# Softmax times values on one core: values of four heads in one load, results of two heads in one store, and another order of the queue

## The chip, the cores and the metric

The kernel runs on one core of one Trainium2 chip. The metric is the device time of one execution in microseconds (us); a median of several executions is quoted with the lowest and highest. Every execution quoted here was fast, that is within 1.5% of the fastest of the same kernel. The span in a profile is that of one profiled execution, from its first to its last instruction, and is about 2 us shorter than the device time of the same execution.

## The reference

```python
# scores: [8, 12, 1024, 1024] float32, v: [8, 12, 1024, 64] float32
def reference(scores, v):
    scores_max = np.max(scores, axis=-1, keepdims=True)
    attn = np.exp(scores - scores_max)
    attn = attn / (np.sum(attn, axis=-1, keepdims=True) + 1e-8)
    return np.matmul(attn, v).astype(np.float32)
```

There are 96 heads. Per head 4 MB of scores and 256 KB of values are read and 256 KB of results are written.

## The kernel before

A loop pass takes four heads. For each head one load brings the values (128 partitions x 2 KiB) and one the scores (128 x 32 KiB). ScalarE (ACT) takes the exponential of two rows per partition at a time and writes it as f16. TensorE (PE) transposes these with an identity into PSUM, VectorE (DVE) copies the transposed row out of PSUM (128 x 1024 f16, 0.69 us), and PE multiplies it with the values. These have a column of ones beside them, so the product brings the row sums too. DVE divides by the sums, and one store per head writes the result.

```python
# s_bufs: 4 x [P, R, SK] f32, v_bufs: 4 x [P, C, D] f32, psO_bufs: 4 x [P, G, M] f32 (PSUM)
def finish(u):                       # one row of a head: products, and after each 4 rows the division
    ...
    if g == G - 1:
        ...
        nc.vector.reciprocal(out=recip[:], in_=psO[:, :, D : D + 1])
        nc.vector.tensor_tensor(out=st["out_sb"][:, r - G + 1 : r + 1, :],
                                in0=psO[:, :, 0:D], in1=recip[:].to_broadcast([P, G, D]), op=mult)
    if r == R - 1:
        dma = nc.sync.dma_start(out=one(out_bh, n), in_=st["out_sb"][:])
        ...
        queue(dma)                   # all transfers stand on one queue, in the order of these calls

def load(k, n, parts=(R,), **cond):
    queue(nc.sync.dma_start(out=v_bufs[k][:], in_=one(v_bh, n), **cond))
    ...                              # then the scores of head n, in one piece or several

def heads(n0):
    for k in range(AHEAD):           # AHEAD = 4 heads
        nc.gpsimd.tensor_copy(out=vones_bufs[k][:, :, 0:D], in_=v_bufs[k][:])
        for r in range(R):           # R = 8 rows per partition
            ...                      # exponential, 8 transposes, copy pt <- psT
            if r == R - 1:
                load_next(k, n0)     # k = 0, 1: loads of heads 0, 1 of the next pass
            ...                      # finish() of the row two before
    load_last(n0)                    # loads of heads 2, 3 of the next pass
```

In the last pass but one the last two score loads are cut into pieces of (4, 4) and (2, 2, 2, 2) rows, so that the last exponentials needn't wait for a whole head.

The softmax here doesn't subtract the row's maximum and nothing guards it: scores larger than these inputs give would overflow.

## Time and profile before

| | before |
|---|---|
| time, median of 4 runs | 1068.95 us (1068.76 to 1069.76) |
| span of the profiled run, granted clock | 1066.77 us, 0.845 |
| transfers in a loop pass of four heads | 12 |
| length of a pass in the middle | 43.9 us |
| last packet of scores ended | 1056.87 us |
| from there to the end of the span | 9.90 us |

The lines of the page that carry this stand in the prediction. In the busy shares, an engine near 100% would be the bound. Here only the DMA engines are, so the middle of the program is paid by the packet. The last two rows of the table are about another stretch: after the last packet nothing is transferred but results.

### The profile page before, as it was taken

How to read it: one execution, taken by the hardware profiler on the slowest of the kernel's cores; microseconds unless marked ns; L12 is line 12 of the kernel's file. 1: busy time of each engine (PE TensorE's matmuls, PEld its weight loads, DVE VectorE, ACT ScalarE, POOL GpSimd, SP SyncE). 2: the span in 40 equal slices, each digit the busy share in tenths (PEclk: the TensorE clock that was granted, in tenths of full speed). 3: DMA queues.
4: the chain of work that ended last, by engine and by line, in shares of the span. 5: the costliest groups of instructions: out<-in, count | busy, mean ns of one | idle time of the engine just before them, and what ended most of it. 6: DMA issues, size and time to landing. Idle time of an engine off the chain costs nothing.

```text
span 1066.8 us, 32321 instructions
## 1 busy us (share of the span) xinstructions
PE 762.6 (71%) x12288; PEld 722.4 (68%) x12288; DVE 609.8 (57%) x1157; ACT 736.3 (69%) x432; POOL 59.9 (6%) x102
## 2 busy tenths in 40 slices
PE   3766767677776777668686777767776777767777
PEld 3766766677776767667676767767666677767766
DVE  2655555555564655656565565655555555555556
ACT  4757676676867768577676766677766767667686
POOL 0000000000000000000000000000000000000000
PEclk9888888878888888987888798887898788888889
DMA  9999999999999999999999999999999999999996
GB/s 402 424 425 426 432 431 421 437 434 424 429 430 435 423 440 428 430 429 420 439 430 433 424 432 435 430 423 427 436 433 424 439 422 429 428 439 429 431 423 265
DMA packets 42051, 453.05 MB, mean 425 GB/s; under 512 B 4672, under 2 KB 4672, under 8 KB 29248
## 3 DMA queue, kind: packets, MB, share of 16 engines
q1 hardware_dynamic: 42048, 453.00, 99.8%
q8 instruction: 3, 0.05, 0.0%
HBM read 436.73 MB, written 25.17 MB: 433 GB/s over the span
## 4 chain that ended last, share of the span: by engine, by line
DMA 49%; PE 20%; PEld 9%; ACT 8%; DVE 7%; issue 3%; SPq 3%; DVEq 0%; ACTq 0%
DMA s_nat<-in_scores_dram 49%; PE psT L190 13%; ACT p_nat L182 8%; PE psO L105 7%; PEld L190 6%; DVE pt L196 5%; PEld L105 3%; DVE out_sb L117 2%; SPq L140 1%; SPq L124 1%; SPq L144 1%; DVE recip L116 0%; SPq L166 0%; DVEq L196 0%; ACTq L182 0%
## 5 line engine op out<-in xcount | busy, mean ns | idle before, releaser
L182 ACT ACTIVATE p_nat<-s_nat 128x2048 f16<-128x2048 f32 (+1 forms) x408 | 705.5, 1800 | 253.5 <-DMA s_nat<-in_scores_dram 130.6
L190 PE MATMUL psT<-ident,p_nat 128*128 128x128 f16 x6144 | 583.9, 254 | 257.0 <-ACT p_nat L182 256.1
L196 DVE COPY pt<-psT 128x1024 f16<-128x1024 f16 x768 | 519.2, 690 | 429.2 <-PE L190 138.2
L190 PEld LDWEIGHTS <-p_nat 128*128 128x128 f16 x6144 | 501.3, 154 | 274.9 <-ACT p_nat L182 271.1
L105 PE MATMUL psO<-vones,pt 128*128 128x65 f16 x6144 | 375.8, 205 | 41.8 <-DVE pt L196 37.5
L105 PEld LDWEIGHTS <-pt 128*128 128x128 f16 x6144 | 309.0, 107 | 64.0 <-DVE pt L196 60.3
L175 POOL CAST vones<-v_sb 128x512 f16<-128x512 f32 x96 | 59.2, 617 | 987.7 <-PE L105 443.7
L117 DVE TENSOR_TENSOR out_sb<-psO,recip 128x256 f32<-128x256 f32 x192 | 80.8, 421 | 4.2
L182 ACT ACT_TABLE_LOAD x24 | 30.8, 1283 | 69.6 <-DMA s_nat<-in_scores_dram 64.8
L116 DVE RECIPROCAL recip<-psO 128x4 f32<-128x4 f32 x192 | 33.4, 174 | 18.0 <-PE psO L105 18.0
L57 DVE MEMSET vones<- 128x8 f16 x4 | 0.2, 65 | 0.8 <-PEq L226 0.8
L51 DVE CAST ident<-ident 128x128 f16<-128x128 f32 x1 | 0.2, 228 | 0.3 <-POOL ident masks.py:199 0.3
masks.py:199 POOL TENSOR_SCALAR_AFFINE_SELECT ident<-ident 128x128 f32<-128x128 f32 x1 | 0.3, 293 | 0.1
masks.py:197 POOL MEMSET ident<- 128x128 f32 x1 | 0.2, 204 | 0.3 <-POOLq L226 0.3
L226 POOL MEMSET const-float32-0.0<- 128x1 f32 x1 | 0.1, 98 | 0.2 <-issue 0.2
L226 POOL MEMSET const-bfloat16-1.0<- 128x1 bf16 x1 | 0.1, 101 | 0.0
L226 POOL MEMSET const-uint8-127<- 128x1 uint8 x1 | 0.1, 101 | 0.0
L226 POOL MEMSET const-float32-1.0<- 128x1 f32 x1 | 0.1, 98 | 0.0
## 6 DMA issues: line engine op xcount, KB each, us to landing
s_nat<-in_scores_dram SPq DMA_DIRECT2D x96, 4096.0 KB, 27.1
v_sb<-in_v_dram SPq DMA_DIRECT2D x98, 256.0 KB, 20.6
out_dram<-out_sb SPq DMA_DIRECT2D x96, 256.0 KB, 18.0
s_nat<-in_scores_dram SPq DMA_DIRECT2D x2, 2048.0 KB, 19.9
s_nat<-in_scores_dram SPq DMA_DIRECT2D x4, 1024.0 KB, 18.7
```

What stands on the lines that cost most here:

```text
L51: nc.vector.tensor_copy(out=ident16[:], in_=ident32[:])
L105: nc.tensor.matmul(out=psO[:, g, :], lhsT=pt[:, c * P : (c + 1) * P], rhs=st["vones"][:, c, :], start=(c == 0), stop=(c == C - 1),)
L116: nc.vector.reciprocal(out=recip[:], in_=psO[:, :, D : D + 1])
L117: nc.vector.tensor_tensor(out=st["out_sb"][:, r - G + 1 : r + 1, :], in0=psO[:, :, 0:D], in1=recip[:].to_broadcast([P, G, D]), op=mybir.Al ...
L124: dma = nc.sync.dma_start(out=one(out_bh, n), in_=st["out_sb"][:])
L140: queue(nc.sync.dma_start(out=v_bufs[k][:], in_=one(v_bh, n), **cond))
L144: nc.sync.dma_start(out=s_bufs[k][:, r : r + rows, :], in_=one(sc_bh, n)[:, r : r + rows, :], **cond,)
L175: nc.gpsimd.tensor_copy(out=vones_bufs[k][:, :, 0:D], in_=v_bufs[k][:])
L182: nc.scalar.activation(out=p_nat[:, g : g + rows, :], in_=s_bufs[k][:, r + g : r + g + rows, :], func=EXP,)
L190: nc.tensor.transpose(out=psT[:, c * P : (c + 1) * P], in_=p_row[:, c, :], identity=ident16[:],)
L196: nc.vector.tensor_copy(out=pt[:], in_=psT[:])
L226: nc = _bacc.Bacc("TRN2", target_bir_lowering=False, num_devices=1)
```

## The change

The intent was to spend fewer, larger packets on values and results, and to keep loads from standing behind stores in the queue. Values of four heads come in one load of 128 x 8 KiB, results leave in stores of 128 x 4 KiB for two heads. The queue of a pass is then: scores 0, scores 1, store of heads 0 and 1, scores 2, values, scores 3, store of heads 2 and 3. That is 7 transfers instead of 12.

The larger packets come at a price in layout. A value load now puts each head on 32 partitions, so after one cast on GpSimd (POOL) 16 DVE copies of 32 x 512 spread a pass's values to their places. A result row pair shares a partition, so the identity of the transposes is permuted and each division writes its two halves of partitions separately.

```diff
-    v_bufs = buffers(sb_pool, AHEAD, [P, C, D], FP32, "v_sb")
+    v_sb = sb_pool.tile([P, S, C, D], FP32, name="v_sb")
+    v_half = sb_pool.tile([P, S, C, D], FP16, name="v_half")
...
-    out_bufs = buffers(sb_pool, 4, [P, R, D], FP32, "out_sb")
+    out_bufs = buffers(sb_pool, 2, [P, T, R, D], FP32, "out_sb")
...
-    psO_bufs = buffers(ps_pool, 4, [P, G, M], FP32, "psO")
+    psO_bufs = buffers(ps_pool, 2, [P, R // G, 512], FP32, "psO")
...
+    def normalise(k, st, first, last):
+        psO = st["psO"][:, first:last, 0 : G * M].rearrange("p b (g m) -> p b g m", m=M)
...
+        for t in range(T):
+            part = slice(t * W, (t + 1) * W)
...
+            nc.vector.tensor_tensor(
...
+        if k == AHEAD - 1:
+            if g == G - 1:
+                normalise(k, st, b, b + 1)
+        elif r == R - 1:
+            normalise(k, st, 0, R // G)
+        if r == R - 1 and k == T - 1:
+            store(n0, 0)
...
+    def spread_v(k):
+        for s in range(S):
+            nc.vector.tensor_copy(
+                out=vones_bufs[k][s * Q : (s + 1) * Q, :, 0:D],
+                in_=v_half[k * Q : (k + 1) * Q, s],
+            )
...
-            loads((R,), (R,))
+            load(AHEAD - 2, (n0 + (2 * AHEAD - 2)) % BH)
+            load_v((n0 + 2 * AHEAD) % BH)
+            load(AHEAD - 1, (n0 + (2 * AHEAD - 1)) % BH)
+            store(n0, AHEAD - T)
...
-                loads((4, 4), (2, 2, 2, 2))
+                load(AHEAD - 2, BH - 2, (4, 4))
+                load(AHEAD - 1, BH - 1, (2, 2, 2, 1, 1))
+                store(n0, AHEAD - T)
```

More of the change, by code (lines that the diff above doesn't have):

```diff
@@ L36 @@
     AHEAD = 4
+    Q = P // AHEAD
+    S = P // Q
+    T = 2
     sc_bh = scores.rearrange("b h (p r) j -> (b h) p r j", p=P)
-    v_bh = v.rearrange("b h (p c) d -> (b h) p c d", p=P)
-    out_bh = out.rearrange("b h (p r) d -> (b h) p r d", p=P)
+    v_bh = v.rearrange("b h (i t) d -> (b h i) (t d)", i=Q)
+    W = P // T
+    out_bh = out.rearrange("b h (j x) d -> (b h j) (x d)", j=W)
     const_pool = ctx.enter_context(tc.tile_pool(name="const", bufs=1))
@@ L49 @@
     make_identity(nc, ident32)
-    ident16 = const_pool.tile([P, P], FP16, name="ident16")
-    nc.vector.tensor_copy(out=ident16[:], in_=ident32[:])
+    order16 = const_pool.tile([P, P], FP16, name="order16")
+    nc.vector.tensor_copy(
+        out=order16[:].rearrange("p (t j) -> p t j", t=T),
+        in_=ident32[:].rearrange("p (j t) -> p t j", t=T),
+    )
     vones_bufs = []
     for k in range(AHEAD):
-        vo = const_pool.tile([P, C, M], FP16, name=f"vones{k}")
-        nc.vector.memset(vo[:, :, D : D + 1], 1.0)
+        vo = const_pool.tile([P, C, D + 2], FP16, name=f"vones{k}")
+        nc.vector.memset(vo[:, :, D : D + 2], 1.0)
         vones_bufs.append(vo)
@@ L65 @@
     s_bufs = buffers(sb_pool, AHEAD, [P, R, SK], FP32, "s_nat")
-    v_bufs = buffers(sb_pool, AHEAD, [P, C, D], FP32, "v_sb")
+    v_sb = sb_pool.tile([P, S, C, D], FP32, name="v_sb")
+    v_half = sb_pool.tile([P, S, C, D], FP16, name="v_half")
     p_bufs = buffers(sb_pool, 8, [P, EB, SK], FP16, "p_nat")
     pt_bufs = buffers(sb_pool, 4, [P, SK], FP16, "pt")
-    out_bufs = buffers(sb_pool, 4, [P, R, D], FP32, "out_sb")
-    rc_bufs = buffers(sb_pool, 4, [P, G, 1], FP32, "recip")
+    out_bufs = buffers(sb_pool, 2, [P, T, R, D], FP32, "out_sb")
+    rc_bufs = buffers(sb_pool, 2, [P, R // G, G, 1], FP32, "recip")
     psT_bufs = buffers(ps_pool, 4, [P, SK], FP16, "psT")
-    psO_bufs = buffers(ps_pool, 4, [P, G, M], FP32, "psO")
+    psO_bufs = buffers(ps_pool, 2, [P, R // G, 512], FP32, "psO")
     turn = {}
@@ L95, in one @@
         return bh[bass.ds(n, 1)].rearrange("o p r d -> (o p) r d")
-    def finish(u):
-        n, r, pt, st = u
-        g = r % G
-        if g == 0:
-            st["psO"] = take(psO_bufs)
-        psO = st["psO"]
+    def normalise(k, st, first, last):
+        psO = st["psO"][:, first:last, 0 : G * M].rearrange("p b (g m) -> p b g m", m=M)
+        recip = st["recip"][:, first:last]
+        nc.vector.reciprocal(out=recip, in_=psO[:, :, :, D : D + 1])
+        h = k % T
+        for t in range(T):
+            part = slice(t * W, (t + 1) * W)
+            rows = st["out_sb"][h * W : (h + 1) * W, t, first * G : last * G, :]
+            nc.vector.tensor_tensor(
+                out=rows.rearrange("j (b g) d -> j b g d", g=G),
+                in0=psO[part, :, :, 0:D],
+                in1=recip[part].to_broadcast([W, last - first, G, D]),
+                op=mybir.AluOpType.mult,
+            )
+    def finish(u):
+        n0, k, r, pt, st = u
+        b, g = r // G, r % G
+        if r == 0:
+            st["psO"], st["recip"] = take(psO_bufs), take(rc_bufs)
+            st["out_sb"] = out_bufs[k // T]
         for c in range(C):
             nc.tensor.matmul(
-                out=psO[:, g, :],
+                out=st["psO"][:, b, g * M : (g + 1) * M],
                 lhsT=pt[:, c * P : (c + 1) * P],
-                rhs=st["vones"][:, c, :],
+                rhs=st["vones"][:, c, 0:M],
                 start=(c == 0),
@@ L111, in finish, with store @@
             )
-        if g == G - 1:
-            if r == G - 1:
-                st["out_sb"] = take(out_bufs)
-            recip = take(rc_bufs)
-            nc.vector.reciprocal(out=recip[:], in_=psO[:, :, D : D + 1])
-            nc.vector.tensor_tensor(
-                out=st["out_sb"][:, r - G + 1 : r + 1, :],
-                in0=psO[:, :, 0:D],
-                in1=recip[:].to_broadcast([P, G, D]),
-                op=mybir.AluOpType.mult,
-            )
-        if r == R - 1:
-            dma = nc.sync.dma_start(out=one(out_bh, n), in_=st["out_sb"][:])
-            for other in stores:
-                apart(dma, other)
-                apart(other, dma)
-            apart(dma, dma)
-            stores.append(dma)
-            queue(dma)
+        if k == AHEAD - 1:
[5 more added lines that the diff above has]
+            store(n0, 0)
+    def store(n0, k):
+        rows = out_bh.rearrange("(m x) y -> m x y", x=P)
+        dma = nc.sync.dma_start(
+            out=rows[bass.ds((n0 + k) // T, 1)].rearrange("o x y -> (o x) y"),
+            in_=out_bufs[k // T][:].rearrange("x t r d -> x (t r d)"),
+        )
+        for other in stores:
+            apart(dma, other)
+            apart(other, dma)
+        apart(dma, dma)
+        stores.append(dma)
+        queue(dma)
     stores = []
@@ L139, in load @@
     def load(k, n, parts=(R,), **cond):
-        queue(nc.sync.dma_start(out=v_bufs[k][:], in_=one(v_bh, n), **cond))
         r = 0
@@ L150, in load, with load_v, cast_v @@
             r += rows
+    def load_v(n):
+        rows = v_bh.rearrange("(m x) y -> m x y", x=P)
+        queue(
+            nc.sync.dma_start(
+                out=v_sb[:].rearrange("x s c d -> x (s c d)"),
+                in_=rows[bass.ds(n // AHEAD, 1)].rearrange("o x y -> (o x) y"),
+            )
+        )
+    def cast_v():
+        nc.gpsimd.tensor_copy(out=v_half[:], in_=v_sb[:])
+    def spread_v(k):
+        for s in range(S):
+            nc.vector.tensor_copy(
+                out=vones_bufs[k][s * Q : (s + 1) * Q, :, 0:D],
+                in_=v_half[k * Q : (k + 1) * Q, s],
+            )
     def load_next(k, n0):
@@ L155, in load_next, with last @@
             load(k, (n0 + (AHEAD + k)) % BH, cond=n0 < BH - AHEAD)
-    def load_last(n0):
+    def last(n0):
         before = queued[-1:]
-        def loads(parts2, parts3):
+        with tc.If(n0 < BH - 2 * AHEAD) as cmp:
             queued[:] = before
-            load(AHEAD - 2, (n0 + (2 * AHEAD - 2)) % BH, parts2)
-            load(AHEAD - 1, (n0 + (2 * AHEAD - 1)) % BH, parts3)
-        with tc.If(n0 < BH - 2 * AHEAD) as cmp:
-            loads((R,), (R,))
+            load(AHEAD - 2, (n0 + (2 * AHEAD - 2)) % BH)
+            load_v((n0 + 2 * AHEAD) % BH)
+            load(AHEAD - 1, (n0 + (2 * AHEAD - 1)) % BH)
+            store(n0, AHEAD - T)
         with cmp.Else():
-            with tc.If(n0 < BH - AHEAD):
-                loads((4, 4), (2, 2, 2, 2))
+            with tc.If(n0 < BH - AHEAD) as cmp2:
+                queued[:] = before
+                load(AHEAD - 2, BH - 2, (4, 4))
+                load(AHEAD - 1, BH - 1, (2, 2, 2, 1, 1))
+                store(n0, AHEAD - T)
+            with cmp2.Else():
+                queued[:] = before
+                store(n0, AHEAD - T)
     def heads(n0):
         for k in range(AHEAD):
-            nc.gpsimd.tensor_copy(out=vones_bufs[k][:, :, 0:D], in_=v_bufs[k][:])
+            spread_v(k)
             st = dict(vones=vones_bufs[k])
@@ L182, in heads @@
                         nc.scalar.activation(
-                            out=p_nat[:, g : g + rows, :],
-                            in_=s_bufs[k][:, r + g : r + g + rows, :],
+                            out=p_nat[:, g : g + rows, :].rearrange(
+                                "p r (s v) -> p s r v", s=S
+                            ),
+                            in_=s_bufs[k][:, r + g : r + g + rows, :].rearrange(
+                                "p r (i s c) -> p s (r i) c", s=S, c=C
+                            ),
                             func=EXP,
@@ L192, in heads @@
                         in_=p_row[:, c, :],
-                        identity=ident16[:],
+                        identity=order16[:],
                     )
@@ L198, in heads @@
                     load_next(k, n0)
-                pending.append((n0 + k, r, pt, st))
+                pending.append((n0, k, r, pt, st))
                 if len(pending) > LAG:
@@ L203, in heads @@
             finish(pending.pop(0))
-        load_last(n0)
-    assert BH % AHEAD == 0 and BH >= 2 * AHEAD
+        cast_v()
+        last(n0)
+    assert BH % AHEAD == 0 and BH >= 2 * AHEAD and SK == Q * S * C
+    load_v(0)
     for k in range(AHEAD):
         load(k, k)
+    cast_v()
+    load_v(AHEAD)
     with tc.For_i(0, BH, AHEAD, iteration_sync="reg_based") as n0:
```

## The prediction

> **What bounds the kernel now.** I read the page's busy shares and its DMA lines first, then the busy time by stretch, the trace's packet records (start, duration and size of every DMA packet), the order of issue on the queue, and last the timeline of the final ten microseconds.
>
> ```profile
> PE 762.6 (71%) x12288; PEld 722.4 (68%) x12288; DVE 609.8 (57%) x1157; ACT 736.3 (69%) x432; POOL 59.9 (6%) x102
> ...
> DMA  9999999999999999999999999999999999999996
> ...
> DMA packets 42051, 453.05 MB, mean 425 GB/s; under 512 B 4672, under 2 KB 4672, under 8 KB 29248
> ...
> q1 hardware_dynamic: 42048, 453.00, 99.8%
> ```
>
> No compute engine is above 71%, while the 16 DMA engines are full in 39 of 40 slices. The packet counts tell what travels: 4672 packets of 4 bytes (16 completions for each of 292 transfers), 29248 - 4672 = 24,576 packets of 2 KiB (values and results, one per partition and head), and 12,800 larger ones (scores, nearly all of 32 KiB).
>
> ```profile
> 500.00:544.00 44.00, 32.51 (x516) 30.72 (x515) 25.37 (x48) 30.78 (x19) 2.47 (x4) 0.81 1.01 429
> 544.00:588.00 44.00, 32.57 (x516) 31.00 (x514) 25.56 (x48) 30.77 (x19) 2.47 (x4) 0.81 1.01 430
> 1000.00:1044.00 44.00, 32.04 (x520) 30.45 (x519) 25.69 (x49) 32.61 (x20) 2.47 (x4) 0.84 1.01 430
> 1044.00:1067.00 23.00, 15.18 (x284) 13.84 (x281) 14.47 (x29) 13.10 (x8) 0.62 (x1) 0.94 0.58 239
> ```
>
> In this table of stretches (busy time of PE, its weight loads, DVE, ACT, POOL, then granted clock, DMA share, GB/s) one loop pass of four heads takes 44 us. The DMA share is 1.01 and the rate 429 to 430 GB/s in each pass; both fall only in the last 23 us. Adding up the packet records gives the same: no idle engine time between 50 and 1050 us, some 7 us per engine in all, nearly all of it after the last score load. So the long middle can shrink only if fewer nanoseconds of packets are put on the engines; a wait taken from a compute engine there is worth nothing.
>
> The order of issue on the queue shows what the change wants to mend:
>
> ```profile
> 1013.30 0.34 SPq L140 DMA_DIRECT2D v_sb<-in_v_dram  x1
> 1014.15 0.33 SPq L144 DMA_DIRECT2D s_nat<-in_scores_dram  x1
> 1014.75 10.07 SPq L124 DMA_DIRECT2D out_dram<-out_sb  x3
> 1025.56 0.35 SPq L140 DMA_DIRECT2D v_sb<-in_v_dram  x1
> ```
>
> Three stores are issued one after the other, over 10 us in which no load is issued. Yet the engines don't run dry, as the shares show: score loads of about 9.7 us each (8 packets of 1.21 us on each engine) still stand in front.
>
> The end hangs on the last landing, which the last two one-row exponentials await:
>
> ```profile
> 1057.39 2.01 ACT L182 ACTIVATE p_nat<-s_nat 128x1024 f16<-128x1024 f32 x2 [0.63 <-PE L105]
> ...
> 1060.96 0.43 PE L105 MATMUL psO<-vones,pt 128*128 128x65 f16 x8 [0.28 <-DVE pt L196]
> 1061.65 0.18 DVE L116 RECIPROCAL recip<-psO 128x4 f32<-128x4 f32 x1 [0.75 <-PE psO L105]
> 1061.87 0.42 DVE L117 TENSOR_TENSOR out_sb<-psO,recip 128x256 f32<-128x256 f32 x1
> ```
>
> The name PE in the first line is the last releaser that the profile saw; the last 8 KiB packet ended at 1056.87, half a microsecond before, so I read it as that DMA's completion. From 1057.4 to the end (1066.8) are 9.4 us: two exponentials, transposes, copy, products, normalising, one store.
>
> **What the Trainium skill says.** "DMA: Bandwidth & Descriptors", section Where 436 GB/s comes from, puts the ceiling of the 16 engines at 435 GB/s. The trace agrees: the packet durations grow by (1213 - 84) ns over (32768 - 2048) bytes, which is 27.2 bytes per ns an engine, 435 GB/s for 16. The same page, section Why small descriptors are slow (HBM only), tells of a fixed overhead of about 3 cycles a packet. The trace agrees in kind: 2 KiB packets follow each other at 80 ns (84 recorded, some 4 overlapped), where 2048 bytes at 27.2 take 75.3; so 4.7 ns a packet, whatever its size (32 KiB at 1209 to 1210 ns fits too). "ScalarE: Activation LUTs", section What ACT_TABLE_LOAD costs, gives an activation one element a cycle plus a constant, 186 + 0.833 x 2048 = 1892 ns; the trace has 1901 ns. "VectorE: DVE Perf Modes", section What auto-detection actually checks, says that a 16-bit one-source copy within SBUF takes the fastest mode; no copy of that kind is in this trace, so the price of the new value copies is an estimate from it.
>
> **The change part by part.**
>
> *Values.* 96 loads of 128 x 2 KiB become 24 of 128 x 8 KiB: 12,288 packets become 3072. Per engine 576 fewer packets x 4.7 ns = 2.7 us. The bytes stay.
>
> *Results.* 96 stores of 128 x 2 KiB become 48 of 128 x 4 KiB. The last 4 heads' stores are issued after the last load in both kernels, so up to the last landing 92 x 128 packets become 46 x 128: 5888 / 16 = 368 fewer per engine x 4.7 = 1.7 us.
>
> *Completions.* 72 + 46 = 118 transfers fewer before the last landing, one score piece more: 117 x 5.5 ns (the spacing of the 4-byte packets) = 0.6 us.
>
> So the last landing should come 5.0 us sooner. As a check, one pass of the loop on one engine: before 32 x 1209.5 + 64 x 80 + 12 x 5.5 = 43.89 us, 430 GB/s, as measured; after 38.70 + 8 x 305.9 ns + 16 x 155.3 ns + 7 x 5.5 ns = 43.67 us, or 432 GB/s, 0.22 us a pass.
>
> *Order of the queue.* Score loads of heads 2 and 3 no longer wait behind the stores. That gives the queue more lead, but there was no idle DMA time for it to take away: 0 us.
>
> *Compute.* POOL casts once per pass instead of four times, the same elements: nothing. DVE gains 16 copies of 32 x 512 f16 per pass. The page's fastest mode gives 512 / 4 / 0.96 = 133 ns, with start some 0.2 us (estimate): 384 x 0.2 = 77 us. In the compiled order all 16 stand at the top of the pass, about 3 us before the first copy out of PSUM. The multiply is split over two halves of the partitions: the measured 421 ns for 256 elements is 267 at one element a cycle plus 154, so 512 elements should take 0.69 us. 144 x 0.69 + 96 x 0.42 = 140 us instead of 81; reciprocals fall from 33 to about 21. DVE goes from 610 to about 610 + 77 + 59 - 12 = 734 us, 69%: still below the DMA, and the 3 us at the top fit in the 11 us or so per pass in which PE idles. ACT reads in runs of 8 elements in another order, with as many elements: 1.9 us as before.
>
> *Tail.* The last score piece is one row instead of two, so one exponential (1.0 us) moves before the last landing. The last head's half is normalised by two multiplies instead of one: +0.4 us. The last store carries two heads: 8 packets of 155 ns on each engine instead of 80: +0.6 us. Sum 0.0: 9.4 us stay.
>
> Sum: 1068.9 - 5.0 + 0.0 = **1063.9 us**, 0.5% faster.
>
> **The rivals.** *Stores next to loads cost more than their packets,* so that keeping them apart gains more. Against it: the 2 KiB packets, loads and stores alike, take 84 ns with hardly an exception; records over the usual duration add up to only 1.5 us per engine, all in the first 65 us. If even that vanished, the time would be 1061 to 1062. *DVE becomes the bound or delays PE,* because the copies run in a slower mode and stand at the top. In the slowest (0.7 us each) they would take 11 us per pass, DVE would be near 85 to 90%, and score buffers would come free late; four score buffers with 27 us from issue to landing absorb some of it. It would make 1070 to 1090; I give it little. *ACT's reordered reading is slower.* With 33 us in 44 it can bear some 30% before it binds; no page or row of this trace speaks for a penalty. At double duration the time would be over 1400. *The tail differs:* some engines finish their last 8 KiB packet almost 2 us after others, which could move the end either way by about 1.5 us.
>
> **Range and chances.** The DMA saving is arithmetic on measured packets (4.5 to 6 us); the early stalls and the unequal engines give about 2 us either way, the tail about 1. So 1060.5 to 1067.0. Faster by 2% would mean 1047.5: the bytes alone at 435 GB/s take 1041, and start and tail add over 10, so almost no chance, 1%. Slower by 2% needs a compute rival: 2%.
>
> **What would show it.** Right: DMA share about 1.01 and 432 GB/s in a middle pass, about 22,000 data packets instead of 37,376, no idle DMA in the middle, a DVE share near 69%, value copies near 0.2 us. Wrong: a DMA share under 0.99 in a middle pass (a compute engine or the queue starves it), 4 KiB packets that take clearly over 159 ns or 8 KiB over 309, exponentials over 1.95 us, or a stretch from last landing to end that isn't near 9.4 us.

## The result

| | before | after | predicted |
|---|---|---|---|
| median | 1068.95 us (4 runs) | 1069.66 us (4 runs, 1069.47 to 1070.16) | 1063.9 (1060.5 to 1067.0) |
| pass in the middle | 43.9 us | 43.67 us | 43.67 us |
| last score packet ended | 1056.87 us | 1050.62 us | 5.0 us sooner |
| from there to the end | 9.90 us | 17.39 us | 9.4 us, unchanged |

The last two score pieces of the changed kernel have one row each and travel in packets of 4 KiB; its last 8 KiB packet ended at 1048.13 (the expectation of e1, with "some 8 us sooner", rests on that one). The prediction's 9.4 us start half a microsecond after the last packet, with the exponentials.

The ratio after to before is 1.0006, with a 95% interval of 0.9989 to 1.0023: the same time. Ratios here are the mean time of one kernel's fast runs over that of the other's of the same rounds, so they are not quite the ratio of the medians quoted. "Same" had a chance of 0.97, so the class came true; the time lies 5.8 us above the predicted one and outside the range.

The first view is the page of the changed kernel: its busy shares, the row of DMA busy tenths, and the packets.

```profile
PE 745.1 (70%) x12288; PEld 706.6 (66%) x12288; DVE 775.8 (73%) x1517; ACT 736.0 (69%) x432; POOL 48.1 (5%) x31
...
DMA  9999999999999999999999999999999999999994
...
DMA packets 24916, 453.06 MB, mean 424 GB/s; under 512 B 2768, under 2 KB 2768, under 8 KB 9168
...
q1 hardware_dynamic: 24912, 453.00, 98.8%
```

The change did what it meant to do to the transfers: 22,144 packets with data (24,912 - 2768) instead of 37,376, and the DMA engines are still full in 39 of 40 slices. DVE rose from 57% to 73%.

The next view is busy time by stretch (PE, weight loads, DVE, ACT, POOL, granted clock, DMA share, GB/s), for two passes in the middle of the changed kernel.

```profile
484.00:528.00 44.00, 31.43 (x512) 29.93 (x512) 32.37 (x64) 30.66 (x18) 1.90 (x1) 0.81 1.00 430
528.00:572.00 44.00, 30.78 (x512) 28.97 (x512) 32.61 (x64) 30.67 (x18) 1.90 (x1) 0.84 1.00 430
```

The DMA engines stay the bound there: a share of 1.00, as before. The packet records show no idle time in the middle, 4 KiB packets of 159 ns and 8 KiB packets of 309 ns. The middle was predicted right. What changed in a pass is DVE: 32.4 us of busy time instead of 25.4.

The queue's timeline of the changed kernel shows the new order in one pass.

```profile
961.82 0.34 SPq L175 DMA_DIRECT2D s_nat<-in_scores_dram  x1
962.51 0.33 SPq L187 DMA_DIRECT2D v_sb<-in_v_dram  x1
973.51 0.33 SPq L175 DMA_DIRECT2D s_nat<-in_scores_dram  x1
980.01 0.36 SPq L153 DMA_DIRECT2D out_dram<-out_sb  x1
989.16 5.18 SPq L175 DMA_DIRECT2D s_nat<-in_scores_dram  x2
```

In the place where the kernel before issued three stores in a row, one store now lies between the scores of head 3 (973.51) and the next pass's scores (989.16).

So the loss is at the end. A pass begins with a table load on ACT, once the pass's first scores have landed. In ACT's timeline this is the last one of the kernel before:

```profile
1023.54 1.28 ACT L182 ACT_TABLE_LOAD   x1 [2.77 <-DMA s_nat<-in_scores_dram]
```

and this the last one of the changed kernel, with most of what ACT does afterwards:

```profile
1020.51 1.28 ACT L240 ACT_TABLE_LOAD   x1 [3.45 <-DMA s_nat<-in_scores_dram]
...
1030.19 22.19 ACT L240 ACTIVATE p_nat<-s_nat 128x2048 f16<-128x2048 f32 x13 [1.07 <-DMA s_nat<-in_scores_dram]
```

The last pass starts 3.03 us sooner. Then 13 exponentials run for 22.19 us with at most 0.1 us between them. The last landing, for which the kernel before waited, is no longer in the chain: the last exponential ends at 1052.38, and DVE copies that row out of PSUM only from 1060.22, 7.8 us later. In the kernel before these are 1059.39 and 1060.21.

What is in the chain is DVE. In the kernel before, its first copy of the last pass was:

```profile
1027.89 0.69 DVE L196 COPY pt<-psT 128x1024 f16<-128x1024 f16 x1 [3.43 <-PE L190]
```

In the changed kernel (DVE's timeline, with one line of PE's between) the last pass starts and ends so:

```profile
1024.77 5.04 DVE L199 COPY vones<-v_half 32x512 f16<-32x512 f16 x16 [0.58 <-PE L252]
1029.84 1.89 DVE L258 COPY pt<-psT 128x1024 f16<-128x1024 f16 x3
...
1060.24 1.18 PE L135 MATMUL psO<-vones,pt 128*128 128x65 f16 x32 [1.53 <-DVE out_sb L120]
...
1062.33 0.18 DVE L115 RECIPROCAL recip<-psO 128x4 f32<-128x4 f32 x1 [1.42 <-PE psO L135]
1062.55 0.88 DVE L120 TENSOR_TENSOR out_sb<-psO,recip 64x256 f32<-64x256 f32 x2
```

The 16 value copies take 5.04 us of DVE, and only then comes the first copy out of PSUM, at 1029.84. The last 32 matmuls, those of the last four rows, wait 1.53 us for a multiply by DVE, although they write another half of the tile than the one it reads.

Put together from these lines, the end moved so:

| stretch | before | after | difference |
|---|---|---|---|
| table load of the last pass begins | 1023.54 | 1020.51 | -3.03 |
| from there to the first copy out of PSUM | 4.35 | 9.33 | +4.98 |
| from there to the end of the last multiply | 34.40 | 33.59 | -0.81 |
| from there to the end of the span | 4.48 | 4.58 | +0.10 |
| span | 1066.77 | 1068.01 | +1.24 |

The 3 us that the DMA side gave were more than taken by one burst of copies on an engine that is idle a quarter of the time.

### The profile page after: what moved, and what is told of

It is laid out like the page before. It is cut to its first block, busy times and chain, and to the rows that moved or that the text cites. A ratio compares the mean times of both kernels' runs of the same rounds, so it can differ in the third digit from the quotient of the medians.

```text
span 1068.0 us, 32453 instructions
## 1 busy us (share of the span) xinstructions
PE 745.1 (70%) x12288; PEld 706.6 (66%) x12288; DVE 775.8 (73%) x1517; ACT 736.0 (69%) x432; POOL 48.1 (5%) x31
## 2 busy tenths in 40 slices
DMA packets 24916, 453.06 MB, mean 424 GB/s; under 512 B 2768, under 2 KB 2768, under 8 KB 9168
## 3 DMA queue, kind: packets, MB, share of 16 engines
q1 hardware_dynamic: 24912, 453.00, 98.8%
## 4 chain that ended last, share of the span: by engine, by line
DMA 78%; ACT 12%; PEld 6%; PE 1%; DVE 1%; issue 1%; SPq 0%; ACTq 0%; DVEq 0%; PEldq 0%
DMA s_nat<-in_scores_dram 78%; ACT p_nat L240 12%; PEld L252 4%; PEld L135 2%; DVE pt L258 1%; PE psT L252 1%; PE psO L135 1%; DVE vones L199 0%; SPq L175 0%; DVE out_sb L120 0%; ACTq L240 0%; SPq L187 0%; DVE recip L115 0%; DVEq L221 0%; PEldq L214 0%
## 5 line engine op out<-in xcount | busy, mean ns | idle before, releaser
L240 ACT ACTIVATE p_nat<-s_nat 128x2048 f16<-128x2048 f32 (+1 forms) x408 | 705.2, 1801 | 226.6 <-DMA s_nat<-in_scores_dram 200.7
L252 PE MATMUL psT<-order,p_nat 128*128 128x128 f16 x6144 | 591.4, 252 | 158.5 <-ACT p_nat L240 150.5
L258 DVE COPY pt<-psT 128x1024 f16<-128x1024 f16 x768 | 511.7, 689 | 221.4 <-PE psO L135 97.8
L135 PE MATMUL psO<-vones,pt 128*128 128x65 f16 x6144 | 354.3, 204 | 157.8 <-DVE pt L258 117.3
L135 PEld LDWEIGHTS <-pt 128*128 128x128 f16 x6144 | 296.1, 106 | 184.9 <-DVE pt L258 136.6
L120 DVE TENSOR_TENSOR out_sb<-psO,recip 64x512 f32<-64x512 f32 (+1 forms) x240 | 139.7, 582 | 7.8
L199 DVE COPY vones<-v_half 32x512 f16<-32x512 f16 x384 | 109.5, 285 | 23.2 <-POOL v_half L194 6.0
L194 POOL CAST v_half<-v_sb 128x2048 f16<-128x2048 f32 x25 | 47.4, 1896 | 994.4 <-DMA v_sb<-in_v_dram 658.3
L115 DVE RECIPROCAL recip<-psO 128x8 f32<-128x8 f32 (+1 forms) x120 | 22.8, 190 | 34.0 <-PE psO L135 34.0
```

Of the source, the lines that this page charges most:

```text
L115: nc.vector.reciprocal(out=recip, in_=psO[:, :, :, D : D + 1])
L120: nc.vector.tensor_tensor(out=rows.rearrange("j (b g) d -> j b g d", g=G), in0=psO[part, :, :, 0:D], in1=recip[part].to_broadcast([W, last ...
L135: nc.tensor.matmul(out=st["psO"][:, b, g * M : (g + 1) * M], lhsT=pt[:, c * P : (c + 1) * P], rhs=st["vones"][:, c, 0:M], start=(c == 0), ...
L194: nc.gpsimd.tensor_copy(out=v_half[:], in_=v_sb[:])
L199: nc.vector.tensor_copy(out=vones_bufs[k][s * Q : (s + 1) * Q, :, 0:D], in_=v_half[k * Q : (k + 1) * Q, s],)
L240: nc.scalar.activation(out=p_nat[:, g : g + rows, :].rearrange("p r (s v) -> p s r v", s=S), in_=s_bufs[k][:, r + g : r + g + rows, :].rea ...
```

## The experiments

The theory after reading the traces: the middle gained what the packets say, and the last pass lost it, by the DVE burst, by the PSUM tile of a head that now spans both halves of its rows, and by the late store of heads 2 and 3 of a pass that is issued behind the next pass's score loads and holds a result buffer. The rivals: the gain of the DMA side isn't there at all (larger packets cost elsewhere), or the last landing still sets the end. Thirteen kernels were run. All outputs are right. The intervals below are some 1.5 us wide to either side. Smaller differences are read from ranges that don't overlap, across rounds whose medians of the kernel before lie between 1068.94 and 1069.11 us, and from the traces.

| run | made from | median us (range) | ratio to before (95%) |
|---|---|---|---|
| e1 | after, copies on GpSimd | 1068.02 (1067.92 to 1068.06) | 0.9991 (0.9978 to 1.0005) |
| e2 | before, values alone | 1154.55 (1152.14 to 1156.27) | 1.0794 (1.0780 to 1.0809) |
| e3 | after, values as before | 1160.53 (1156.45 to 1163.05) | 1.0855 (1.0835 to 1.0874) |
| e4 | before, order of stores alone | 1122.95 (1120.83 to 1125.35) | 1.0511 (1.0496 to 1.0526) |
| e5 | e4 and one dummy load | 1084.44 (1084.10 to 1084.65) | 1.0143 (1.0128 to 1.0159) |
| e6 | e2 and one dummy load | 1069.92 (1068.75 to 1070.16) | 1.0005 (0.9991 to 1.0019) |
| e7 | e3 and two dummy loads | 1086.04 (1085.42 to 1086.60) | 1.0157 (1.0143 to 1.0171) |
| e8 | e1, two PSUM tiles, store sooner | 1065.55 (1065.18 to 1065.82) | 0.9966 (0.9952 to 0.9980) |
| e9 | e8, copies back on DVE | 1069.38 (1068.88 to 1069.98) | 1.0004 (0.9990 to 1.0018) |
| e10 | after, two PSUM tiles | 1068.10 (1067.72 to 1068.57) | 0.9994 (0.9981 to 1.0008) |
| e11 | e6, copies on GpSimd | 1068.43 (1068.16 to 1068.89) | 0.9997 (0.9983 to 1.0010) |
| e12 | e11, last rows in pieces of one | 1068.74 (1068.44 to 1068.80) | 0.9998 (0.9984 to 1.0011) |
| e13 | e8, store where it was | 1067.36 (1067.24 to 1067.46) | 0.9984 (0.9970 to 0.9998) |

### e1: the value copies on GpSimd

```diff
-            nc.vector.tensor_copy(
+            nc.gpsimd.tensor_copy(
                 out=vones_bufs[k][s * Q : (s + 1) * Q, :, 0:D],
```

> The changed kernel with one edit: the 16 value copies of each pass run on GpSimd instead of DVE. Backlog theory (A): the changed kernel's middle passes did become 0.2 us shorter and its last load lands some 8 us sooner, but in the last pass DVE is late: 5.04 us of copies in one burst ahead of the first copy out of PSUM (1024.77 to 1029.81), then 33.6 us of work without a wait for data. With the burst gone the last pass starts its DVE chain some 4 to 5 us sooner: 1064 to 1066 us, DVE share near 62%. Order rival (B): moving the stores behind the loads is what costs, not DVE: 1069 to 1070 as the changed kernel. Tail rival (C): the wait of the last head's products for its own first multiply (1.5 us) and the doubled last store and multiply eat the gain: 1069 or so, 0 to 1 us gained.

Measured: 1068.02 us, 1.64 below the changed kernel. The first copy out of PSUM in the last pass came at 1024.50, that is 5.34 us sooner, but the end of the span came only 2.21 us sooner. The timeline of e1 (DVE and PE) shows where the rest went:

```profile
1052.45 1.41 DVE L120 TENSOR_TENSOR out_sb<-psO,recip 64x512 f32<-64x512 f32 x2 [2.22 <-DMA out_dram<-out_sb]
...
1054.64 0.43 PE L135 MATMUL psO<-vones,pt 128*128 128x65 f16 x8 [2.76 <-DVE pt L258]
```

The multiply of head 94 waits 2.22 us for the landing of a store: that of heads 90 and 91, whose buffer it writes, and which stands in the queue behind the last score pieces. PE stands idle for 2.76 us with it. So the burst was in the chain, and behind it stood the next wait. The time lies outside the range of each of the three theories; after the wait the granted clock is 0.50 from 1056 us to the end, and the last 32 matmuls take 1.92 us instead of 1.18.

### e2, e3, e4: each part by itself

e2 is the kernel before with the value part of the diff alone (one load of four heads, one cast, 16 DVE copies, the reordered exponentials). Its queue has 9 transfers per pass. The core of its edit, against the kernel before:

```diff
-        queue(nc.sync.dma_start(out=v_bufs[k][:], in_=one(v_bh, n), **cond))
...
+            if more:
+                load_v((n0 + 2 * AHEAD) % BH)
```

> The kernel before with only the value part of the change: one load for four heads, 16 DVE copies at the top of each pass; stores, their order and the multiplies as before. Backlog theory (A): the DMA saving is 576 x 4.7 ns + 72 x 5.5 ns = 3.1 us up to the last landing, a pass takes 43.75 us, but the burst of 5.0 us sits ahead of the last pass's chain on DVE and the tail grows by 3 to 5 us: 1068 to 1071 us. B and C, for which the copies are harmless: 1065.5 to 1066.5.

e3 is the changed kernel with the values as before, one load per head, and the exponentials' old order of reading; 10 transfers per pass. Against the changed kernel:

```diff
+        queue(nc.sync.dma_start(out=v_bufs[k][:], in_=one(v_bh, n), **cond))
...
-            spread_v(k)
+            nc.gpsimd.tensor_copy(out=vones_bufs[k][:, :, 0:D], in_=v_bufs[k][:])
```

> The changed kernel with its values loaded and cast as in the kernel before: only the paired stores, their place in the queue, and the split multiplies. Backlog theory (A): DMA saves 368 x 4.7 ns + 46 x 5.5 ns = 2.0 us; no burst, so the last pass isn't late by 5 us, only by the longer multiplies: 1065.5 to 1068. Tail rival (C): all of the loss is here: 1069 to 1072. Order rival (B): likewise 1069 or more.

e4 is the kernel before with its stores in other places: those of heads 0 and 1 together after the loads of head 1, those of heads 2 and 3 after the loads of head 3; still 12 transfers per pass.

```diff
-            dma = nc.sync.dma_start(out=one(out_bh, n), in_=st["out_sb"][:])
...
+            done.append(st["out_sb"])
+            if len(done) == 2:
+                store(n - 1, done[0])
+                store(n, done[1])
...
+        def late():
+            store(n0 + 2, done[2])
+            store(n0 + 3, done[3])
```

> The kernel before with only the queue's order changed: the stores of heads 0 and 1 after the second load, those of heads 2 and 3 after the fourth; sizes as before. A: bytes and packets are the same, a middle pass stays 43.9 us, the last score load lands 2 to 4 us sooner because four stores move behind it, and the end gains what the last pass's computation can follow: 1066.5 to 1069. B: the order itself costs: over 1069.5.

All three missed by far: 1154.55, 1160.53 and 1122.95 us. Parts of a change that together cost nothing cost 5 to 8.5% each. The first question was what the queue waits for. First the queue's own waits in e4 (line, what it waits for: us in total, number, longest), then two lines of its timeline, the values and scores of head 0 of one pass:

```profile
SPq L151 <- DMA s_nat<-in_scores_dram: 352.5, 46, 9.7
```

```profile
490.25 0.36 SPq L147 DMA_DIRECT2D v_sb<-in_v_dram  x1
499.96 0.35 SPq L151 DMA_DIRECT2D s_nat<-in_scores_dram  x1
```

Score loads are held back until another score load has landed: 46 waits, two for each of 23 passes, of up to 9.7 us, the time of one whole score load. So the scores of head 0 are issued 9.7 us after the values. The data don't ask for that. The built program does: it has eight completion semaphores for the queue (the issues in e4's trace carry the numbers 113 to 120, here 0 to 7), given to the transfers in turn, and a transfer that takes a semaphore waits for the landing of the earlier transfer on it. In e4:

```
order of a pass    v0 s0 v1 s1 st0 st1 v2 s2 v3 s3 st2 st3
semaphore (of 8)    0  1  2  3   4   5  6  7  0  1   2   3
s3 waits on semaphore 1 for the landing of s0; s0 of the next pass for that of s3
```

The scores of head 3 are the last load in the queue, so when they have landed the queue holds no load. In the kernel before, with the same 12 transfers, the one that shares with s3 is the value load of head 1, and the values and scores of head 0 and a store already stand in the queue by then. In e2 (9 per pass) the first transfer shares with the ninth, which is s3 again; in e3 (10 per pass) the first value load shares with s3. The changed kernel has 7 per pass, so no two transfers of a pass share one.

Busy time by stretch (same columns as above), for e4 and then e2, shows the cost in a middle pass:

```profile
484.00:528.00 44.00, 31.46 (x511) 29.81 (x510) 24.83 (x48) 29.22 (x18) 2.47 (x4) 0.84 0.98 407
```

```profile
484.00:528.00 44.00, 28.39 (x462) 27.01 (x459) 27.51 (x60) 27.24 (x16) 1.90 (x1) 0.83 0.96 392
```

The rate falls from 429 to 430 GB/s to 407 and 392 (416, and 395 to 405, in the stretches beside these), and a pass of e4 takes about 45.6 us. By the packet records, from 50 us to about a pass before the last loads, an engine is idle for 8 us in e4, 50 in e2 and 37 in e3. Beside the idle time, packets are slow: the first after a gap (625 ns longer than the usual 1213 on average at 455 us of e4), and packets of 32 KiB some 18 to 20 us later, by 0.5 to 1.0 us. Slow packets add 31 us per engine in e4, 38 in e2 and 36 in e3. Why the later ones are slow stays open.

### e5, e6, e7: the same parts with dummy loads that shift the turn

If sharing a semaphore is the cause, one transfer of 1 KB more per pass, which shifts the turn, must give the time back although it adds work. If the order, or the larger packets as such, is the cause, it can't. The fillers are loads of 16 x 16 f32 that nobody reads:

```diff
+    pad_sb = sb_pool.tile([16, 16], FP32, name="pad_sb")
+    def pad():
+        queue(nc.sync.dma_start(out=pad_sb[:], in_=v[0, 0, 0:16, 0:16]))
...
                 store(n - 1, done[0])
                 store(n, done[1])
+                pad()
```

This is e5, made from e4. In e6, made from e2, one filler stands after the store of head 1. In e7, made from e3, two stand after the first store.

> The order-only kernel (1122.95 us) plus one filler transfer per pass, a load of 16 x 64 bytes that nothing reads, behind the stores of heads 0 and 1. Completion theory (D): the queue's issuer waits, before it issues a transfer, for the landing of the earlier one that uses the same of eight completion semaphores. In the order-only kernel the first score load of a pass shares its semaphore with the score load issued last, so the queue runs dry once a pass (0.3 us idle, 0.6 us for the first packets after it, 0.7 us of stretched packets some 19 us later). The filler shifts the sharing by one: 1066.5 to 1070 us, no idle DMA time in the middle, 43.9 us a pass. Rival (B), the order of stores and loads is itself what costs: 1120 or more, the filler only adds work.

> The values-only kernel (1154.55 us) plus one filler transfer behind the store of head 1. D: nine transfers a pass put the first and the ninth, both score loads, on one completion semaphore; with ten the first shares with the value load instead. Back to 1066 to 1070 us: the DMA saving of 3.1 us minus what the DVE burst of 5 us at the top of the last pass costs. Rival: the value load of 8 KiB rows, or the DVE copies, make it slow in themselves: 1150 or so.

> The stores-only kernel (1160.53 us) plus two filler transfers behind the first store. D: ten transfers a pass put the first value load on the semaphore of the last score load; twelve move that meeting to the second value load, behind 10 us of other work. 1065 to 1069 us. Rival: paired stores with the split multiply cost in themselves: 1155 or more.

Measured: 1084.44, 1069.92 and 1086.04 us, that is 38.5, 84.6 and 74.5 us less than without fillers. Idle time and slow packets of e4, e2 and e3 had added up to 39, 88 and 74 us. e6 met its expectation; e5 and e7 gave most of the time back but missed theirs. Busy time by stretch in e6:

```profile
484.00:528.00 44.00, 32.19 (x520) 30.48 (x518) 29.92 (x65) 30.66 (x18) 1.90 (x1) 0.81 1.00 429
```

The pass is back at a DMA share of 1.00, with 43.77 us a pass in e6, as its packets add up to (32 x 1209.5 + 8 x 305.9 + 32 x 80 + 10 x 5.5 ns), and the middle has no idle engine time in e5, e6 and e7. So the sharing is shown to be the cause of what the fillers gave back, of the 85.6, 91.5 and 54.0 us that e2, e3 and e4 had lost. The value part alone, once freed of it, costs what the whole change costs: 1069.92 against 1069.66.

e5 and e7 keep some 15 to 17 us. Those lie nearly all at the end, as ACT's timeline of e5 shows:

```profile
1058.32 14.62 ACT L203 ACTIVATE p_nat<-s_nat 128x2048 f16<-128x2048 f32 x9 [16.14 <-DMA out_dram<-out_sb]
```

ACT waits 16.14 us for the landing of a store before it may go on with the last pass. In the branch for the last pass but one, with its cut score loads, the first piece of head 94 and the last store have the same semaphore (number 0) in the built programs of e5 and e7, so that wait reads as the same thing in another place. That reading wasn't tried with a run of its own.

### e8, e9, e13, e10: dividing the tail

e8 adds two mends to e1: the two halves of the last head of a pass go to two PSUM tiles, and in the last pass but one the late store is issued before the last score pieces.

```diff
+        psO, bank = st["psO"], b
+        if k == AHEAD - 1:
+            psO, bank = psO_bufs[1 - b], 0
...
                 load(AHEAD - 2, BH - 2, (4, 4))
-                load(AHEAD - 1, BH - 1, (2, 2, 2, 1, 1))
                 store(n0, AHEAD - T)
+                load(AHEAD - 1, BH - 1, (2, 2, 2, 1, 1))
```

> The kernel with the value copies on GpSimd (1068.02 us) with two more edits: the last head's two halves are summed in two PSUM tiles, so that its second half doesn't wait for the multiply of its first (1.5 us in the profile), and in the last pass but one the store of heads 2 and 3 is issued before the last score pieces, so that its landing doesn't hold up the multiply of head 2 in the last pass (2.2 us, and 2.9 us of PE after which its clock is half). Tail theory (A, mended): all that the DMA saves is there at the last landing and is eaten by these three: 1063 to 1065.5. Rival: the last pass's DVE work, 33 us without waits, binds anyway: 1067 to 1068.

e9 is e8 with the copies on DVE again:

```diff
-            nc.gpsimd.tensor_copy(
+            nc.vector.tensor_copy(
```

> The three-mended kernel (1065.55 us) with the value copies put back on DVE, as in the changed kernel. Backlog theory (A): the 5.04 us burst at the top of the last pass is back, with nothing else in the way: 4 to 5 us more, 1069 to 1070.5, the first copy out of PSUM of the last pass near 1030 us. Rival: only the two other mends matter, the burst is hidden beside ACT's first exponentials of the pass: 1065.5 to 1066.5.

e13 is e8 without the store's move:

```diff
                 load(AHEAD - 2, BH - 2, (4, 4))
-                store(n0, AHEAD - T)
                 load(AHEAD - 1, BH - 1, (2, 2, 2, 1, 1))
+                store(n0, AHEAD - T)
```

> The kernel with the value copies on GpSimd (1068.02 us) with the two PSUM tiles for the last head, but the store of heads 2 and 3 left behind the last score pieces, as in the changed kernel. If both remaining mends count: the wait of the last pass's multiply for that store's landing (2.2 us) is still there and only the 1.5 us of the PSUM tile are gained, 1066.3 to 1066.9, between 1068.02 and 1065.55. If the store's place gave nothing: 1065.3 to 1065.8. If the PSUM tile gave nothing here: 1067.7 to 1068.1.

e10 is the changed kernel with the two PSUM tiles and nothing else:

```diff
+        psO, bank = st["psO"], b
+        if k == AHEAD - 1:
+            psO, bank = psO_bufs[1 - b], 0
```

> The changed kernel with one edit: the last head's two halves are summed in two PSUM tiles. The wait of 1.53 us that PE had for the multiply of the first half falls away at the very end: 1 to 1.6 us less than the changed kernel's 1069.66, so 1068.0 to 1068.7. If the tail isn't on this wait: 1069.5.

Measured: e8 1065.55, e9 1069.38, e13 1067.36, e10 1068.10 us. DVE's timeline of the last pass, first e9 and then e8:

```profile
1024.68 5.04 DVE L206 COPY vones<-v_half 32x512 f16<-32x512 f16 x16 [0.58 <-PE psT L259]
1029.75 0.69 DVE L265 COPY pt<-psT 128x1024 f16<-128x1024 f16 x1
```

```profile
1025.30 2.02 DVE L265 COPY pt<-psT 128x1024 f16<-128x1024 f16 x3 [0.47 <-PE L259]
...
1057.87 0.88 DVE L124 TENSOR_TENSOR out_sb<-psO,recip 64x256 f32<-64x256 f32 x2
```

The multiply of head 94 shows the store's place, first in e13 and then in e8:

```profile
1052.47 1.41 DVE L124 TENSOR_TENSOR out_sb<-psO,recip 64x512 f32<-64x512 f32 x2 [1.85 <-DMA out_dram<-out_sb]
```

```profile
1050.26 1.41 DVE L124 TENSOR_TENSOR out_sb<-psO,recip 64x512 f32<-64x512 f32 x2
```

From e9 to e8 the first copy out of PSUM moves from 1029.75 to 1025.30, by 4.45 us, and the time by 3.83 us. This is one edit of one word, so the burst's price is shown. In steps, from the changed kernel: copies off DVE 1.64 us, two PSUM tiles 0.66 more (e1 to e13), the store's place 1.81 more (e13 to e8); 4.11 in all. The steps don't simply add in another order. The two PSUM tiles alone give 1.56 us (e10), and adding the store's move to that, with the copies on DVE (e9), takes 1.28 away again: the first copy out of PSUM came 1.28 us later (1029.75 against 1028.47). At head 91's exponentials ACT waits 6.00 us in e8 and 6.07 in e9, for a store's landing, against 4.84 in e10, for the scores. So the sooner store seems to have a side cost there, which no run of its own tested. e9, e10 and, within 0.1 us, e8 did as expected; e13 lies between its ranges, so both mends count, the store's place more. e8 beats both kernels, by 3.4 us against the one before. It is still 1.65 us above the predicted time, and this remainder isn't divided; in its last pass an exponential starts 0.11 us after the landing of its scores (1049.86), and PE waits 0.88 us for it, so a landing is in the chain again.

### e11, e12: does the end hang on the last landing?

e11 is e6 (stores as before, one load of values, one filler) with the copies on GpSimd. e12 is e11 with the last two rows in pieces of one, so that the last landing releases less work.

```diff
-                loads((4, 4), (2, 2, 2, 2), False)
+                loads((4, 4), (2, 2, 2, 1, 1), False)
```

> The values-with-filler kernel (1069.92 us) with the value copies on GpSimd. Its stores, multiplies and PSUM tiles are those of the kernel before, so only the DVE burst stands between it and its DMA saving of 3.1 us. A: 1065 to 1066.5. If the burst is not what cost it: 1069 to 1070.

> The same with the last score piece cut into one row and one row, as in the changed kernel: the exponential of row 6 moves before the last landing. If the end still hangs on that landing: 0.5 to 1.0 us less than the one before, 1064 to 1066. If the end hangs on DVE's work instead: no difference within 0.3 us.

Measured: 1068.43 and 1068.74 us. e12 shows that smaller last pieces give nothing: the last multiply ended at 1062.27 against 1062.32 in e11. e11 itself missed its expectation. Its passes grew from 43.78 to about 44.0 us from about 590 us on (in e12 from about 455, and in the kernel before, from 43.89, from about 630), so its last pass started only at 1025.04, against 1022.60 in e6. From there to the end of the span it took 41.35 us, the shortest of all; the kernel before took 43.23 and the changed one 47.50. So its tail is better than that of the kernel before by 1.9 us, and slower passes took that away. The landing records show where the growth sits. Each transfer has 16 completions, one per DMA engine, and has landed with the last of them. In e11 the first and the last lie 2.95 us apart until 540 us and 5.2 us at the end (medians over 60 us; 2.60 throughout in e6, 2.34 and then 3.08 in the kernel before). It is one engine that falls behind: of a transfer at 987 us in e11, fifteen completions came within 2.95 us and the sixteenth after 4.99. Why it does stays open.

## Why the prediction was right or wrong

**What bounds the kernel: right, for the middle.** The DMA engines stayed full, the pass took 43.67 us as worked out, and the packets took their predicted times. The rival that stores beside loads cost more than their packets is not borne out: e6, with the old stores and their order, ran its passes at the length of its packets.

**Five us on the DMA side: right in mechanism, one store miscounted.** The last score packet ended 6.25 us sooner. One more pair of heads than the prediction counted, 90 and 91, is stored behind the last score piece (45 stores before it, where the prediction had 46), which makes 8 packets of 155 ns, 1.24 us; 5.0 and 1.24 are 6.24. At the start of the last pass the count fits too: by then 93 value loads and 88 stores have become 24 and 44. On one engine that is 181 x 8 x 80 ns = 115.8 us against 24 x 8 x 305.9 + 44 x 8 x 155.3 ns = 113.4 us, and 113 fewer completions at 5.5 ns are 0.6 us. The sum is 3.1 us; the table load came 3.03 us sooner. Part of that match is luck: by then one engine of the kernel before was some 0.7 us behind, which the count leaves out.

**"Order of the queue ... 0 us": right for this program, but for too simple a reason.** No idle time was there to be taken away. But e2 to e4 show that order and number can put idle time there, up to 8.5%. The parts aren't worth what they are worth together: 7 transfers in a pass are fewer than the 8 semaphores.

**"POOL casts once per pass ...: nothing" and the exponentials: right.** The cast takes 1896 ns once a pass. An exponential of 128 x 2048 took 1.90 us in its new order of reading.

**The cost of the value copies: mis-sized.** The groups of the changed kernel (busy us and mean ns of one, then idle time before) have both new costs of DVE:

```profile
L120 DVE TENSOR_TENSOR out_sb<-psO,recip 64x512 f32<-64x512 f32 (+1 forms) x240 | 139.7, 582 | 7.8
L199 DVE COPY vones<-v_half 32x512 f16<-32x512 f16 x384 | 109.5, 285 | 23.2 <-POOL v_half L194 6.0
```

The multiplies are right (140 us predicted, 139.7 measured), the reciprocals nearly (21 and 22.8). A copy took 285 ns rather than "some 0.2 us". The Trainium skill has the number: "VectorE: DVE Perf Modes", section Side-by-side: where the cycles go for N=2048 bf16, counts some 150 cycles of start and 8 of fill beside the elements. For 512 elements at four a cycle that is (128 + 158) / 0.96 = 298 ns, an estimate which this trace confirms within 5%. The prediction had added only some 70 ns to its 133. So 109.5 us instead of 77, and the burst at the top is 5.04 us instead of "about 3 us". It accounts for 32.5 of the 42 us by which DVE's 776 exceed the predicted 734.

**The step that failed: "Sum 0.0: 9.4 us stay", and with it "the 3 us at the top fit in the 11 us or so per pass in which PE idles".** The idle time is there because compute waits for data: on the page of the changed kernel PE's transposes wait 150.5 us for ACT, and of ACT's 226.6 us of idle time before its exponentials 200.7 are put down to the landing of scores. In the last pass, from 1030.19 on, the data come before compute can use them, and this idle time no longer exists. There DVE's work and its waits count, at the top of the pass (3.83 us, e8 against e9), at the division (two PSUM tiles, 1.56 us, e10) and in the wait for a buffer (1.81 us, e8 against e13). These three prices, each from its own pair of runs, don't simply add: all three mends together gave 4.11 us. So from the last landing to the end it became 17.4 us instead of 9.9. That is 7.5 us more, and with the last landing 1.25 us sooner than forecast, the span ended 6.2 us later than the 1066.77 - 5.0 us forecast. The prediction had named one form of the DVE rival, the slow mode with late score buffers in the middle, and gave it little. DVE did delay the chain, but in the last pass alone and without score buffers coming late.

**"The end hangs on the last landing": true of the kernel before only by some 2 us.** Its last pass took 43.23 us from table load to end, and e11, with the same stores and divisions and an end that smaller last pieces didn't move (e12), does it in 41.35. A landing sooner than that could give at most this difference (an estimate from these two spans). Beyond it, only an earlier start of the last pass helps: 3.03 us here. Even with a tail without loss, the change was worth about 3 to 5 us rather than whatever the last landing gained; e8 got 3.4.

## What to carry to other kernels

In a kernel bound by transfers, follow a saving to the last instruction: in the last pass there may be little left to await from memory, as here, and then work that hid in idle time of an engine (a burst of small copies, a wait for half of a tile, a buffer held by a late store) comes due in full. Put such work on an engine with nothing to do, and keep what two engines touch in separate tiles. And when the order or number of transfers in a loop changes, look at which transfers share a completion semaphore, before explaining the time by the order itself.

## What the Trainium skill lacked or had wrong

- "DMA: Bandwidth & Descriptors", section Why a DMA increments its semaphore by 16 and not by 1, warns of two transfers in flight on one semaphore because the count can then mislead, and advises one semaphore per slot in flight. It does not tell what a program pays that waits instead, as these built programs do: 54 to 92 us of 1069 (e4, e2, e3 against the kernel before), of which one or two dummy loads of 1 KB took 38 to 85 us back.
- "DMA: Bandwidth & Descriptors", section Why small descriptors are slow (HBM only), gives the overhead of a packet in cycles, with an example of 256 bytes, and no time for it. Here it fits 4.7 ns for each packet, whether of 2 KiB or of 32 KiB.
- No page was found on packets that become slower after the queue has run dry: 32 KiB packets were 0.5 to 1.0 us longer some 18 to 20 us later (e2, e4). The cause is open.
- No page was found on one of the 16 DMA engines falling behind within a run, so that landings come later: first and last completion 2.95 and then 5.2 us apart in e11, passes of 43.78 and then about 44.0 us. The cause is open.
